# q split in the projections, low parts of weights kept in DRAM, attention's scores three units ahead: a hybrid decoder layer on one core

## The chip, the core and the metric

One Trainium2 chip, one of its cores. The time is device microseconds (us) of one execution; each figure is the median of several runs. TensorE (PE) multiplies matrices, with its weight load shown apart as PEld; VectorE (DVE), ScalarE (ACT) and GpSimd (POOL) work element by element; SyncE (SP) issues most DMAs. Each engine works through its own instructions in order.

## What is computed

A decoder layer over 2048 tokens of width 1024, in fp32:

```python
h = rmsnorm(x, g);  proj = h @ w_in                        # 1024 -> 3328
y_a = rwkv7_mixer(proj[:, :1792], ...)                     # 8 heads of 64, a recurrence in chunks
y_b = dilated_attention(q, k, v)                           # 8 heads of 64
x = x + concat(y_a, y_b) @ w_out
h = rmsnorm(x, ffn_g)
x = x + (silu(h @ w_gate) * (h @ w_up)) @ w_down           # 1024 -> 2816 -> 1024
return rmsnorm(x, final_g)
```

The attention runs three times per head and mixes the results by their log-sum-exp: in windows of 128 tokens, in windows of 512 over every 4th token, and over the whole sequence over every 16th. A query sees its own block of 128 keys and the one before it.

## The kernel before, in words

**Split products.** Each fp32 factor of a dense product is split into a high part `hi`, its value in the rounded format fp32r (`nc.scalar.copy`, ACT), and a low part `lo = raw - hi` (`tensor_tensor`, DVE). `three` (L234 to L237) makes hi x hi, lo x hi and hi x lo. For attention's scores a head's q (64 rows) is loaded twice, into partitions 0 to 63 and 64 to 127; `split_q` (L937) leaves its high part in partitions 0 to 63 and its low part in 64 to 127; k, loaded twice too, is split by `split_k` (L942) into two such tiles, so that two matmuls (L968, L969) make a score.

**Weights.** `Weights` (L186) serves pieces of 256 KB (128 x 512): `load` issues the raw load on SP (two raw buffers), `halve` splits it into `whi` and `wlo` (three buffers each), `take` hands out the next and keeps one more split ahead. A piece serves 12 matmuls. For `w_in` the first block of tokens also stores both parts in DRAM by POOL (L224), and the other three blocks read both back on SP (L205 to L211). All other weights, 416 pieces, are split every time: `w_out` once or more per block, `w_gate`, `w_up` and `w_down` in two passes over the tokens (`list_out`, `list_down`, L1400 to L1424), and `w_down` for the last two blocks from another `Weights` (`wds`).

**The order.** PE's instructions stay in the order of the program; the other engines' are ordered by a scheduler. The work is generators that yield costs in us. `drive` (L155) runs two of them against each other: each step of the first kind (rwkv, later attention) gives so many us to the second (the dense products). First the projections of four blocks of 512 tokens run with rwkv (`dense_in`, to about 820 us): 26 column tiles per block, of which tiles 14 to 17 are q, 18 to 21 k, 22 to 25 v. q and k go to DRAM, transposed, as `qT` and `kT`. Then attention runs against the output projections and the FFN.

**Attention.** The parts follow in `heads_b`: `attention(0)`, `branch3` (the 16-fold dilation, all blocks), `attention(1)` to `attention(3)`. `prep(h)` splits a head's operands: in `attention` q and k once in order (`q1`, `kh1`, `kl1`) and once reordered by 4 (`q2`, `kh2`, `kl2`), in `branch3` four blocks reordered by 16. A `Unit` is the score matmuls of one to four tiles into one of two PSUM buffers, a row maximum on DVE (L973, a subtraction of it follows in ACT's exponential, L978), transpositions into one PSUM buffer (L985), a copy from there by ACT or DVE in turn (L989), and the products with v (L999), copied out by ACT (L1004) and POOL (L1005). `flow` (L1012) puts the scores of a unit `ahead=2` units in front of its transpositions. Where there is a second buffer for k (`spare`, from the end of rwkv to the end of `attention(1)`) the next head's `prep` runs beside the units (`sides`), else between heads.

**The dense side.** `start` and `start_b` make output projections of blocks 0 to 3 from y_a and y_b: `put_by` (L1622) loads four tiles of x on SP, adds the products and stores the sums to `x1p`. Then `normed` (L1486) squares, scales and transposes block 0 in ten steps; each yields `HOLD` = 1.6 us to attention. `chunks0` and `chunks1` are the FFN of blocks 0 and 1, with `put_rest` (L1743) for the rest of the projections and `prepare` for blocks 2 and 3, whose gate products (`gate_up_pair`, 2300 to 2710 us) and down products (`downs`) come last; `next_acts` (L1982) loads the activations of a chunk from DRAM (`actD`) and splits them.

Of the kernel before, what the change touches and what calls it, by code (L numbers as in the profile page):

```python
# [9 lines left out]
F32 = mybir.dt.float32  # L10
# [31 lines left out]
def f32(ap):  # L42
    return ap.bitcast(F32)
# [3 lines left out]
def tile_hybrid_layer(  # L47
# [41 lines left out]
    qT = dram.tile([W, S], F32, name="qT")  # L89
# [96 lines left out]
    class Weights:  # L186


        def __init__(self, pool, srcs, raw_bufs, bufs, kept=None, again=0):


            self.pool, self.srcs, self.raw_bufs, self.bufs = pool, srcs, raw_bufs, bufs
            self.kept, self.again = kept, again or len(srcs)
            self.raw, self.ready, self.loaded, self.split = [], [], 0, 0

        def load(self):
            if self.loaded < self.again:
                src = self.srcs[self.loaded]
# [5 lines left out]
        def halve(self):  # L204
            if self.again <= self.split < len(self.srcs):  # L205
                parts = []
                for n, name in enumerate(("whi", "wlo")):
                    t = self.pool.tile([P] + list(self.srcs[self.split].shape[1:]), F32R, name=name, tag=name, bufs=self.bufs)
                    nc.sync.dma_start(out=f32(t), in_=self.kept[self.split % self.again, n])
                    parts.append(t)  # L210
                self.ready.append(tuple(parts))  # L211
                self.split += 1
            elif self.split < len(self.srcs):
                while self.loaded <= self.split:
                    self.load()
                raw = self.raw.pop(0)
                hi = self.pool.tile(list(raw.shape), F32R, name="whi", tag="whi", bufs=self.bufs)
                nc.scalar.copy(out=hi, in_=raw)  # L218
                lo = self.pool.tile(list(raw.shape), F32R, name="wlo", tag="wlo", bufs=self.bufs)
                nc.vector.tensor_tensor(out=lo, in0=raw, in1=f32(hi), op=ALU.subtract)  # L220
                self.ready.append((hi, lo))
                if self.kept is not None:
                    for n, t in enumerate((hi, lo)):
                        nc.gpsimd.dma_start(out=self.kept[self.split, n], in_=f32(t))  # L224
                self.split += 1
                while self.loaded < self.split + self.raw_bufs - 1 and self.loaded < self.again:
                    self.load()

# [17 lines left out]
    A_TAIL, A_START, A_FIRST, A_REST, HOLD = 0.5, 0.6, 1.14, 1.15, 1.6  # L246
# [87 lines left out]
    def new_suv():  # L334
# [3 lines left out]
    n_in = 2 * len(ORDER)  # L338
    w_parts = dram.tile([n_in, 2, P, 4, P], F32, name="w_parts")
# [3 lines left out]
            w_in2[half * 512 : (half + 1) * 512, ct * P : (ct + 1) * P].rearrange("(k p) n -> p k n", p=P)  # L343
            for _ in range(NB) for ct in ORDER for half in range(2)
        ],
        2, 3,
        w_parts, n_in,
# [38 lines left out]
    def dense_in():  # L386
# [58 lines left out]
        for b in range(nblocks):  # L445
            t0 = b * TB
            for at, ct in enumerate(ORDER):
# [26 lines left out]
                if ct < SHIFT_TILES:  # L474
# [28 lines left out]
                    got[b, ct] = o  # L503
                else:
                    o = sp.tile([P, TB], F32, name="qkv", bufs=1)
                    nc.scalar.copy(out=o, in_=pd)
                    if ct < 22:
                        dst = qT if ct < 18 else kT
                        r0 = ((ct - 14) % 4) * P
                        nc.scalar.dma_start(out=dst[r0 : r0 + P, t0 : t0 + TB], in_=o)  # L510
# [501 lines left out]
    def flow(units, ahead=2):  # L1012
# [83 lines left out]
    def attention(b):  # L1096
# [27 lines left out]
        def load_qk(h):  # L1124
            hs = slice(h * HD, (h + 1) * HD)
            rq = ap.tile([P, TB], F32, name="rq", tag="rq", bufs=2)
            load_dup(rq, qT[hs, t0 : t0 + TB])
# [929 lines left out]
```

## Time and profile before

| | |
|---|---|
| median of 3 runs | 2978.59 us (2977.94 to 2982.78) |
| profiled execution, its own time | 2977.17 us |
| its span, first to last instruction | 2975.1 us |
| mean granted TensorE clock | 0.98 |
| busy: PE, PEld | 2844.0 us (96%), 2333.9 us (78%) |
| busy: DVE, ACT, POOL | 2013.0 us (68%), 1329.4 us (45%), 610.0 us (21%) |
| DMA | 443.63 MB, mean 149 GB/s |

Busy time is that of instructions at work; waiting is not in it. Matmuls overlap, so one's duration is longer than the distance to the next. The granted clock is a share of 2.4 GHz; a mean of 0.9 is a stretch in which a fifth of the time was at 1.2 GHz. Waits are inferred: a line "A <- B" says that an instruction of A started late, and that what it last waited for was B. An engine may also be late without such a wait, when an instruction ahead of it in its queue is.

### The profile page before, as it was taken

What the parts mean: (1) busy time and instruction counts of PE and PEld (TensorE: products, weight loads), DVE (VectorE), ACT (ScalarE), POOL (GpSimd) and SP (SyncE); (2) the same over time, 40 slices, a digit from 0 to 9 for tenths busy, and PEclk for the clock granted to TensorE, in tenths of its full rate; (3) what the DMA queues carried; (4) which work ended last, traced back from release to release, by engine and by line L of the source; (5) the groups of instructions that cost most, each with busy time, mean ns of one, the idle gap of its engine ahead of it and who ended that gap; (6) DMA issues with size and microseconds to landing.
All of it is one profiled execution on the core that took longest, in us unless ns stands there. A gap on an engine that the chain in (4) does not pass through costs nothing. (4 is left out here: it accounts for less than half of the span.)

```text
span 2975.1 us, 47453 instructions
## 1 busy us (share of the span) xinstructions
PE 2844.0 (96%) x17193; PEld 2333.9 (78%) x17193; DVE 2013.0 (68%) x3970; ACT 1329.4 (45%) x2568; POOL 610.0 (21%) x801
## 2 busy tenths in 40 slices
PE   7999999999998888899999999999988999999998
PEld 6777777877777777788888888888776788887887
DVE  6776667667568877766666687665458777776443
ACT  5533423423326665665545566453244333334332
POOL 4443112113113222000111121111012333330001
PEclk9999999999998998899999999999999999999999
DMA  7673564553453787454445544443564322224443
GB/s 247 215 226 125 159 182 135 161 179 124 135 171 96 230 245 229 136 145 116 134 138 142 146 126 137 142 112 100 182 193 145 125 81 82 81 72 173 151 145 101
DMA packets 398158, 443.63 MB, mean 149 GB/s; under 512 B 31282, under 2 KB 264292, under 8 KB 397924
## 3 DMA queue, kind: packets, MB, share of 16 engines
q1 hardware_dynamic: 347124, 358.20, 40.3%
q0 software_dynamic: 18144, 59.78, 5.4%
q10 hardware_dynamic: 32656, 22.62, 2.5%
q8 instruction: 136, 2.23, 0.3%
q14 instruction: 98, 0.80, 0.1%
HBM read 351.03 MB, written 89.46 MB: 148 GB/s over the span
## 5 line engine op out<-in xcount | busy, mean ns | idle before, releaser
L220 DVE TENSOR_TENSOR wlo<-wraw,whi 128x512 fp32r<-128x512 f32 x468 | 331.1, 709 | 364.0 <-ACT whi L218 358.0
L218 ACT CAST whi<-wraw 128x512 fp32r<-128x512 f32 x468 | 289.2, 619 | 495.2 <-PE acc L237 217.7
L235 PE MATMUL pd<-h_hi,whi 128*128 128x512 f32 (+1 forms) x840 | 351.0, 418 | 2.0 <-DVE kx L483 0.9
L236 PE MATMUL pd<-h_lo,whi 128*128 128x512 f32 (+1 forms) x840 | 330.2, 393 | 1.0 <-DVE h_lo L403 0.8
L237 PE MATMUL pd<-h_hi,wlo 128*128 128x512 f32 (+1 forms) x840 | 330.4, 393 | 0.0
L1005 POOL COPY oo<-mx 128x2 f32<-128x2 f32 (+2 forms) x160 | 54.2, 345 | 767.3 <-DVE mx L973 644.6
L978 ACT ACTIVATE pr<-pr,mx 128x256 f32<-128x256 f32 (+1 forms) x416 | 162.7, 450 | 90.6 <-DVE mx L973 90.1
L235 PEld LDWEIGHTS pd<-h_hi,whi 128*128 128x128 f32 x840 | 159.5, 190 | 37.5 <-DVE kx L483 1.4
L237 PEld LDWEIGHTS pd<-h_hi,wlo 128*128 128x128 f32 x840 | 159.3, 190 | 35.4
L236 PEld LDWEIGHTS pd<-h_lo,whi 128*128 128x128 f32 x840 | 159.9, 190 | 28.6 <-DVE h_lo L403 2.6
L237 PE MATMUL mm<-z,wlo 128*128 128x512 f32 x440 | 174.7, 397 | 0.6 <-DVE wlo L1905 0.6
L236 PE MATMUL mm<-z,whi 128*128 128x512 f32 x440 | 174.4, 396 | 0.0
L235 PE MATMUL mm<-z,whi 128*128 128x512 f32 x440 | 174.2, 396 | 0.0
L999 PEld LDWEIGHTS po<-vv,pts 128*128 128x128 f32 x1008 | 152.6, 196 | 23.9 <-ACT oo L1004 4.3
L1924 DVE TENSOR_TENSOR part<-mm,part 128x512 f32<-128x512 f32 x154 | 105.7, 686 | 91.8 <-PE mm L237 91.8
L973 DVE CUSTOM_DVE_ANT_0 pr<-s_att,amask 128x256 f32<-128x256 f32 (+1 forms) x384 | 122.0, 361 | 47.5 <-PE s_att L969 46.8
L1903 ACT CAST whi<-raw 128x512 fp32r<-128x512 f32 x110 | 68.2, 621 | 189.9 <-PE mm L236 186.4
L235 PE MATMUL acc<-whi,a_hi 128*128 128x512 f32 x352 | 149.7, 425 | 3.0 <-DVE th L1521 1.3
L235 PE MATMUL acc<-whi,fh_hi 128*128 128x512 f32 x320 | 140.3, 438 | 11.0 <-ACT whi L218 5.1
L235 PE MATMUL pg<-fh_hi,whi 128*128 128x512 f32 x352 | 148.4, 422 | 0.6 <-DVE x L1538 0.6
L235 PE MATMUL pu<-fh_hi,whi 128*128 128x512 f32 x352 | 148.3, 421 | 0.0
L999 PE MATMUL po<-vv,pts 128*128 128x65 f32 x1008 | 144.5, 268 | 3.1 <-ACT oo L1004 3.1
(646 smaller groups left out, 7267.0 us busy)
## 6 DMA issues: line engine op xcount, KB each, us to landing
wraw<-in_w_down_dram SPq DMA_DIRECT2D x176, 256.0 KB, 2.8
whi<-w_parts SPq DMA_DIRECT2D x156, 256.0 KB, 2.7
wlo<-w_parts SPq DMA_DIRECT2D x156, 256.0 KB, 3.3
wraw<-in_w_gate_dram SPq DMA_DIRECT2D x88, 256.0 KB, 3.2
wraw<-in_w_up_dram SPq DMA_DIRECT2D x88, 256.0 KB, 2.8
rq<-qT SPq DMA_DIRECT2D x128, 128.0 KB, 3.3
wraw<-in_w_out_dram SPq DMA_DIRECT2D x64, 256.0 KB, 4.9
wraw<-in_w_in_dram SPq DMA_DIRECT2D x52, 256.0 KB, 3.7
```

What stands on the lines that cost most here:

```text
L218: nc.scalar.copy(out=hi, in_=raw)
L220: nc.vector.tensor_tensor(out=lo, in0=raw, in1=f32(hi), op=ALU.subtract)
L235: nc.tensor.matmul(ps, lhsT=lhs[0], rhs=rhs[0], start=first, stop=False)
L236: nc.tensor.matmul(ps, lhsT=lhs[0], rhs=rhs[1], start=False, stop=False)
L237: nc.tensor.matmul(ps, lhsT=lhs[1], rhs=rhs[0], start=False, stop=last)
L973: nc.vector.tensor_tensor_reduce(out=pr[:, g, :], in0=ps[:, g, :], in1=mask, scale=-0.125, scalar=-NEG, op0=ALU.add, op1=ALU.min, accum_ou ...
L978: nc.scalar.activation(out=pr[:, g, :], in_=pr[:, g, :], func=AF.Exp, scale=-1.0, bias=mx[:, g])
L999: nc.tensor.matmul(po[:, g, :], lhsT=pts[:, g, kb, :], rhs=vb[g][kb], start=(kb == 0), stop=(kb == kbs - 1))
L1005: nc.gpsimd.tensor_copy(out=o[:, :, OA:OW], in_=self.mxs[j])
L1903: nc.scalar.copy(out=hi, in_=raw)
L1924: nc.vector.tensor_tensor(out=out, in0=ps, in1=other, op=ALU.add)
```

## The change

- **q.** The projections split a q tile once (hi on ACT from PSUM, lo on DVE) and store both to `qS`. Attention loads the two halves into the two halves of the partitions; `split_q` is gone. The reordered copies, of q in all branches and of k's two parts in `attention`, are made by `nc.gpsimd.tensor_copy` (`turned_by`). k in `attention` is split once over the longer range. `branch3` still splits k in reordered form.
- **Low parts.** `Weights` takes for each piece where to store parts and where to read them. `w_in` stays as it was. Of the other pieces the first use of `w_gate`, `w_up`, `w_down` and the second half of `w_out` stores the low part by POOL (140 pieces); each later use (244 pieces) loads it on SP into the `wlo` buffer, without the DVE subtraction. The high part is still cast from the raw piece.
- **Order.** `flow` runs `ahead=3`; `HOLD` is 2.2, and the first norm yields three more of them after its first scaled half. `put_by` and `put_rest` load their residual rows after half of the pieces. `next_acts` loads two pairs of activations and then one more pair for every two that are split.

```diff
-    qT = dram.tile([W, S], F32, name="qT")
+    qS = dram.tile([2, W, S], F32, name="qS")
...
         def halve(self):
+            if self.split == len(self.srcs):
+                return
+            src, put, have = self.srcs[self.split]
+            shape = [P] + list(src.shape[1:])
+            hi = self.pool.tile(shape, F32R, name="whi", tag="whi", bufs=self.bufs)
+            lo = self.pool.tile(shape, F32R, name="wlo", tag="wlo", bufs=self.bufs)
+            for part, kept in zip((hi, lo), have or ()):
+                if kept is not None:
+                    nc.sync.dma_start(out=f32(part), in_=kept)
+            if not have or have[0] is None:
+                while self.loaded <= self.used:
                     self.load()
                 raw = self.raw.pop(0)
+                self.used += 1
                 nc.scalar.copy(out=hi, in_=raw)
+                if not have:
+                    nc.vector.tensor_tensor(out=lo, in0=raw, in1=f32(hi), op=ALU.subtract)
+                while self.loaded < self.used + self.raw_bufs - 1 and self.loaded < len(self.raws):
                     self.load()
+            for part, kept in zip((hi, lo), put or ()):
+                if kept is not None:
+                    nc.gpsimd.dma_start(out=kept, in_=f32(part))
...
-    A_TAIL, A_START, A_FIRST, A_REST, HOLD = 0.5, 0.6, 1.14, 1.15, 1.6
+    A_TAIL, A_START, A_FIRST, A_REST, HOLD = 0.5, 0.6, 1.14, 1.15, 2.2
...
+                elif ct < 18:
+                    hi = sp.tile([P, TB], F32R, name="q_hi", tag="qkv", bufs=1)
+                    lo = sp.tile([P, TB], F32R, name="q_lo", tag="kx", bufs=2)
+                    nc.scalar.copy(out=hi, in_=pd)
+                    nc.vector.tensor_tensor(out=lo, in0=pd, in1=f32(hi), op=ALU.subtract)
+                    r0 = (ct - 14) * P
+                    for n, part in enumerate((hi, lo)):
+                        nc.scalar.dma_start(out=qS[n, r0 : r0 + P, t0 : t0 + TB], in_=f32(part))
...
-    def split_q(hi, raw):
-
-        nc.scalar.copy(out=hi, in_=raw)
-        nc.vector.tensor_tensor(out=hi[HD:P], in0=raw[HD:P], in1=f32(hi[HD:P]), op=ALU.subtract)
+    def load_q_parts(dst, h, ts):
+
+        for n in range(2):
+            nc.sync.dma_start(out=f32(dst[n * HD : (n + 1) * HD]), in_=qS[n, h * HD : (h + 1) * HD, ts])
+
+    turned_by = nc.gpsimd.tensor_copy
...
-    def flow(units, ahead=2):
+    def flow(units, ahead=3):
...
-            split_q(q1, rq)
-            split_k(kh1, kl1, rk_all[:, TB - lead :])
+            turned_by(out=q1, in_=rq)
+            turned_by(out=q2, in_=rq.rearrange("p (i r) -> p r i", r=4))
+
+            kh, kl = place[:, 0, 0:n2], place[:, 1, 0:n2]
+            split_k(kh, kl, rk_all[:, TB - back :])
+            kh1, kl1 = kh[:, n2 - n1 :], kl[:, n2 - n1 :]
             yield 0.0
...
-            split_q(q2, rq.rearrange("p (i r) -> p r i", r=4))
-            split_k(kh2, kl2, rk_all[:, TB - back :].rearrange("p (n i r) -> p r n i", r=4, i=P))
+            for o, k in ((kh2, kh), (kl2, kl)):
+                turned_by(out=o, in_=k.rearrange("p (n i r) -> p r n i", r=4, i=P))
...
-                split_q(q3[:, :, b * n : (b + 1) * n], qs.pop(0).rearrange("p (i r) -> p r i", r=R3))
+                turned_by(out=q3[:, :, b * n : (b + 1) * n], in_=qs.pop(0).rearrange("p (i r) -> p r i", r=R3))
...
+    def list_one(key, src, again=False):
+
+        if not again:
+            srcs.append((src, None, None))
+        elif key in lows:
+            srcs.append((src, None, (None, lows[key])))
+        else:
+            lows[key] = dram.tile([P] + list(src.shape[1:]), F32, name=f"low{len(lows)}")
+            srcs.append((src, (None, lows[key]), None))
...
-    def normed(x1, b, h, hold):
+    def normed(x1, b, h, hold, lead=0):
...
                     loaded.append((ht, h, i, kq))
+                    if not i and not kq:
+                        for _ in range(lead):
+                            yield hold
                 yield hold
...
-            xts = []
-            for i in range(NT):
-                xt = fp.tile([P, W], F32, name="xh", tag="a_hi", bufs=6)
-                nc.sync.dma_start(out=xt, in_=x2[b * TB + i * P : b * TB + (i + 1) * P, ds_])
-                xts.append(xt)
             acc = [ps_f.tile([P, 512], F32, name="acc", tag="f") for _ in range(NT)]
             for n, k in enumerate(ks):
                 wh = wf.take()
+                if n == len(ks) // 2:
+                    xts = []
+                    for i in range(NT):
+                        xt = fp.tile([P, W], F32, name="xh", tag="a_hi", bufs=6)
+                        nc.sync.dma_start(out=xt, in_=x2[b * TB + i * P : b * TB + (i + 1) * P, ds_])
+                        xts.append(xt)
...
-        yield from normed(x1s[0], 0, hs_[0], HOLD)
+        yield from normed(x1s[0], 0, hs_[0], HOLD, 3)
...
+        load()
+        load()
         act = [(hi[:, f], lo[:, f]) for f in range(f1 - f0)]
...
-        for hi_f, lo_f in act:
+        for n, (hi_f, lo_f) in enumerate(act):
+            if n % 2 == 0:
+                load()
             nc.scalar.copy(out=hi_f, in_=f32(lo_f))
```

## Rows read from the trace of the kernel before

**Rows 1.** The page, first part: busy time, share of the span, instructions.
```profile
PE 2844.0 (96%) x17193; PEld 2333.9 (78%) x17193; DVE 2013.0 (68%) x3970; ACT 1329.4 (45%) x2568; POOL 610.0 (21%) x801
```
**Rows 2.** Windows by stage: length, busy us and instructions per engine, clock, DMA share, GB/s.
```profile
225.00:825.00 600.00, 590.29 (x4863) 470.35 (x4860) 403.12 (x816) 220.46 (x463) 132.12 (x153) 1.00 0.48 150
885.00:975.00 90.00, 70.36 (x756) 61.15 (x756) 76.81 (x209) 59.22 (x140) 33.39 (x49) 0.81 0.37 109
975.00:1125.00 150.00, 132.05 (x753) 111.17 (x753) 117.94 (x320) 97.07 (x206) 31.48 (x55) 0.94 0.81 243
1125.00:1275.00 150.00, 124.54 (x702) 108.07 (x701) 108.67 (x279) 100.24 (x193) 17.16 (x31) 0.89 0.59 175
1275.00:2175.00 900.00, 893.34 (x4741) 753.37 (x4740) 587.32 (x1210) 454.71 (x840) 115.08 (x175) 1.00 0.47 137
2175.00:2325.00 150.00, 134.32 (x585) 106.23 (x584) 108.55 (x173) 68.80 (x136) 31.66 (x32) 0.97 0.51 165
2325.00:2700.00 375.00, 375.00 (x1613) 303.03 (x1612) 276.88 (x345) 117.72 (x194) 137.07 (x116) 1.00 0.25 80
2700.00:2775.00 75.00, 70.14 (x294) 56.03 (x293) 44.05 (x69) 29.72 (x51) 2.18 (x4) 0.95 0.60 212
```
**Rows 3.** PE's waits from 885 to 1275: us in total, times, longest.
```profile
PE pt_att L985 <- DVE pts L989: 9.1, 6, 4.3
PE pt_att L985 <- ACT pts L989: 8.6, 6, 4.1
...
PE ptf L1445 <- DVE ht L1500: 5.5, 1, 5.5
PE s_att L968 <- ACT k_all L943: 4.7, 1, 4.7
PE s_att L968 <- DVE q2nd L940: 4.3, 1, 4.3
PE ptf L1445 <- DVE fh_lo L1448: 3.9, 4, 1.9
PE s_att L968 <- DVE mx L973: 3.6, 3, 1.3
```
**Rows 4.** The timeline, 1061 to 1067: start, us, engine, instruction, [idle before <- releaser].
```profile
1061.37 2.87 DVE L940 TENSOR_TENSOR q1st<-rq,q1st 64x512 fp32r<-64x512 f32 x2
1061.42 2.00 POOL L1363 TENSOR_TENSOR c<-oo,aog 128x512 f32<-128x512 f32 x1 [0.81 <-DVE oo L1358]
...
1064.61 1.27 ACT L978 ACTIVATE pr<-pr,mx 128x128 f32<-128x128 f32 x4 [5.10 <-DVE mx L973]
...
1066.41 0.66 PE L985 MATMUL pt_att<-ident,pr 128*128 128x128 f32 x4 [2.20 <-ACT pts L989]
```
**Rows 5.** The q subtractions (L940) from 885 to 1275: DVE busy us, clock, DMA.
```profile
885.00:1275.00 390.00, 51.01 (x51) 0.89 0.62 186
```
**Rows 6.** DVE's instructions by line and form, whole span: busy us, mean ns, idle before.
```profile
L220 DVE TENSOR_TENSOR wlo<-wraw,whi 128x512 fp32r<-128x512 f32 x468 | 331.1, 709 | 364.0 <-ACT whi L218 358.0 <-PE s_att L969 2.7 <-PE pt_att L985 1.9
...
L1905 DVE TENSOR_TENSOR wlo<-raw,whi 128x512 fp32r<-128x512 f32 x110 | 74.8, 680 | 0.1
...
L944 DVE TENSOR_TENSOR k_all<-rk_all,k_all 128x1024 fp32r<-128x1024 f32 x20 | 40.4, 2021 | 15.6 <-ACT k_all L943 15.6
```
**Rows 7.** POOL's instructions by line and form, whole span.
```profile
L224 POOL DMA_DIRECT2D w_parts<-wlo x52 | 28.9, 555 | 22.8 <-DVE wlo L220 10.4 <-DVE up L710 2.8 <-DVE M L714 2.6
...
L724 POOL MEMSET TAB<- 32x1024 f32 x8 | 7.6, 948 | 29.5 <-ACT TAB L723 29.2
```
**Rows 8.** The timeline at 2400, in the paired gate products.
```profile
2399.51 1.62 POOL L1896 TENSOR_TENSOR S<-S,raw 128x512 f32<-128x512 f32 x1
...
2400.51 1.18 DVE L1905 TENSOR_TENSOR wlo<-S,whi 128x512 fp32r<-128x512 f32 x1
```
**Rows 9.** PE's waits from 2215 to 2295.
```profile
PE acc L236 <- DVE wlo L220: 4.7, 3, 2.8
```
**Rows 10.** The page, sixth part: DMA issues, KB each, median us to landing.
```profile
wlo<-w_parts SPq DMA_DIRECT2D x156, 256.0 KB, 3.3
```

More of the change, by code (lines that the diff above doesn't have):

```diff
@@ L186, in tile_hybrid_layer, with __init__ @@
     class Weights:
-        def __init__(self, pool, srcs, raw_bufs, bufs, kept=None, again=0):
+        def __init__(self, pool, srcs, raw_bufs, bufs):
             self.pool, self.srcs, self.raw_bufs, self.bufs = pool, srcs, raw_bufs, bufs
-            self.kept, self.again = kept, again or len(srcs)
-            self.raw, self.ready, self.loaded, self.split = [], [], 0, 0
+            self.raws = [n for n, (_, _, have) in enumerate(srcs) if not (have and have[0] is not None)]
+            self.raw, self.ready, self.loaded, self.split, self.used = [], [], 0, 0, 0
         def load(self):
-            if self.loaded < self.again:
-                src = self.srcs[self.loaded]
+            if self.loaded < len(self.raws):
+                src = self.srcs[self.raws[self.loaded]][0]
                 raw = self.pool.tile([P] + list(src.shape[1:]), F32, name="wraw", tag="wraw", bufs=self.raw_bufs)
@@ L204, in halve @@
         def halve(self):
[L205 to L214, printed above, removed]
+            if self.split == len(self.srcs):
+                return
@@ L229, in take @@
+            self.ready.append((hi, lo))
+            self.split += 1
         def take(self):
@@ L1754, in put_rest @@
                 wh = wf.take()
+                if n == len(ks) // 2:
+                    xts = []
+                    for i in range(NT):
+                        xt = small("xr")
+                        nc.sync.dma_start(out=xt, in_=x1p[b * TB + i * P : b * TB + (i + 1) * P, ds_])
+                        xts.append(xt)
                 for i in range(NT):
@@ L1991, in next_acts, with load @@
             hi, lo = (pair_tile(t, 8) for t in tags)
-        for f in range(f0, f1, 2):
-            nc.sync.dma_start(
-                out=f32(lo[:, f - f0 : f - f0 + 2]), in_=actD[b, f : f + 2].rearrange("f p t -> p f t")
-            )
+        todo = list(range(f0, f1, 2))
+        def load():
+            if todo:
+                f = todo.pop(0)
+                nc.sync.dma_start(
+                    out=f32(lo[:, f - f0 : f - f0 + 2]), in_=actD[b, f : f + 2].rearrange("f p t -> p f t")
+                )
+        load()
+        load()
         act = [(hi[:, f], lo[:, f]) for f in range(f1 - f0)]
```

62 lines of the change are left out of this document (22 added, 40 removed).

## The prediction

> **What bounds the kernel now.** The profiled execution took 2977.17 us: a span of 2975.1 and 2.07 around it; the median of the runs shown, 2978.59, lies 1.4 above. The page's first part gives TensorE (PE) 2844.0 us of the span [rows 1], so at most 131 us can be won without less matmul work, and the change takes no matmul away. The windows by stage say where the 131 us lie [rows 2]. From 885 to 1275, where the first attention block and the dilation-16 branch run beside the output projections and the first norm, PE is idle for 19.64 + 17.95 + 25.46 = 63 us. There its granted clock is 0.81, 0.94 and 0.89, so it spent 2 x (0.19 x 90 + 0.06 x 150 + 0.11 x 150) = 85 us at 1.2 of 2.4 GHz. A stream at half clock lasts twice as long: up to 43 us more. From 1275 to 2175 PE is busy 893 of 900 us: nothing done for another engine there can show. From 2175 to 2325 it idles 16 us, from 2700 to 2775 5 us.
>
> PE's waits in that first stage name the engines behind it [rows 3]. The transposition waits 17.7 us for copies of the previous one out of its single PSUM buffer, the scores 12.6 us for their operands or PSUM (4.7 + 4.3 + 3.6), the norm's transpositions 9.4 us for DVE. One stretch of the timeline shows how [rows 4]: DVE spends 2.87 us on two q subtractions, the row maxima come after them, ACT stands 5.10 us at the exponentials, the copy behind these in ACT's queue comes late, and PE stands 2.20 us. So this stage hangs on the queues of DVE and ACT: DVE is busy 76.81 + 117.94 + 108.67 = 303 of 390 us.
>
> **The change, part by part.**
> *q split once.* In attention every head's q was split anew: 51 subtractions of 51.0 us on DVE in this stage [rows 5], each with a cast on ACT. All go. So does one of two k splits per head of attention(0), about 1 us by half of the 128x1024 row [rows 6], 8 us. Relief: 59 of DVE's 303 us, and about as much on ACT. It costs a subtraction and one more store for each of 16 q tiles in the projections: 16 x 0.709 = 11 us of DVE [rows 6], and ACT's queue can stand as long at the second store. PE is busy 590 of 600 us there [rows 2], and a tile's 24 matmuls cover the step: 375 us for 1613 matmuls [rows 2] make 0.232 us each, 5.6 us per tile. Without that cover it would cost those 11 us. I take 1.
>
> *POOL makes the reordered copies.* In place of the splits stand 64 POOL copies of 512 columns in this stage (four per head of attention(0) and of branch3). The trace has no such copy. The nearest rows are a memset of 1024 columns, 0.948 us, so 0.47 for 512 [rows 7], and a sum of two operands, 1.62 [rows 8]; I take 1.0, one operand read in strides lying between them, so 64 us; ends 30 and 104. POOL has room. The later blocks add 24 heads at 6 such copies' worth, 144 us in 900, where POOL was busy 115 [rows 2].
>
> POOL's work has a price on DVE, though [rows 8]. At 2400.51 a DVE subtraction with both operands in SBUF lasts 1.18 us while a POOL sum runs from 2399.51 for 1.62; undisturbed it takes 0.680 [rows 6]. It ended 0.56 us after the sum: it stood until POOL was done. The q subtraction in the timeline stretched in the same way, beside a POOL product of 2.00 us [rows 4]. If a quarter of the copies' 64 us stands in front of DVE, 16 us of the relief are given back: 59 - 16 = 43.
>
> The Trainium skill's GPSIMD Engine Reference (section 7) counts 2.9 cycles per element for reads in steps of over 8 bytes and 1.9 for others; at its 1.2 GHz that would be, as an estimate, 1.24 and 0.81 us, 76 us for the 64 copies. No row shows it.
>
> The Trainium skill's SBUF — State Buffer (section Terms) calls the port pair that the two engines share locked for a whole instruction, so that the loser fully blocks; the rows agree (1.18 us against 0.680). By that rule the extreme is a DVE held for all of POOL's time: a rival below.
>
> DVE's busy share falls from 303/390 = 0.78 to 260/390 = 0.67. Delay in a queue grows as busy over free time, 3.5 before and 2.0 after: some 45% less. Of the 30.3 us of operand and copy waits (17.7 + 12.6) that is **14 us**.
>
> *Three units ahead.* The scores' matmuls move one unit forward in PE's fixed order; nothing is added. ACT's and DVE's row work gets one unit more of time, the case of [rows 4]. It helps what the 45% covers, and some of the 23 us of idle time that [rows 3] do not name: **3 us**. The "pr" tiles (5 buffers) then hold five at most in attention(0), so DVE's maxima of a next unit can wait for the transpositions right before it; these stand ahead of it on PE, so this costs nothing.
>
> *The first norm.* After the first scaled half, attention now gets 4 x 2.2 = 8.8 us where it had 1.6: 7.2 more in front of a transposition that waited 5.5 us [rows 3]. I take that wait whole, and of 3.9 us behind it 2.5: **8 us**. The work comes from the full stage behind, which gets as much shorter.
>
> *Clock.* 14 + 3 + 8 = 25 of 63 us idle, 40%. The half-speed time follows the idle stretches: 40% of 43 is 17, and as PE often waits there anyway, half: **9 us**; ends 0 and 17.
>
> *Low parts kept.* 140 weight pieces are stored by POOL, and 244 are read later in place of a DVE subtraction of 0.709 us, 173 us of DVE. Nearly all of that lies where PE is full (893 of 900), so it is hidden and worth nothing. The exception is the preparation around 2250, where PE waits 4.7 us for a low part [rows 9]: **4 us**. The stores take 140 x 0.555 = 78 us of POOL [rows 7]; a store that is late holds one of three "wlo" buffers, so the subtraction three pieces on, then PE. The projections' first block does it with two stores per piece on the same three buffers. I take 1, ends 0 and 30.
>
> The reads are tighter. A low part's load waits on SP until its buffer is free, two pieces before its use: 24 matmuls, 5.6 us where no attention stands between. Such a load lands in 3.3 us [rows 10], which leaves 2.3. Behind it on SP stand the next raw piece, whose cast still has a piece more, and attention's loads, which come a head ahead. I take 2, ends 0 and 40.
>
> *Loads moved.* The residual rows of put_by and put_rest leave SP behind two weight pieces in place of ahead of all, so weights no longer stand behind their waits for buffers; they then have two pieces, 5.6 us without attention, until the sums. I take 2 for put_rest, where nothing else covers them, ends -3 and 8. The activation loads of the last stage come in pairs in place of all at once; around 2720 that relieves SP, but low parts now queue behind the token loads. PE idles 5 us there [rows 2]; I take 0, ends -5 and +8. Slower two-operand work on DVE under PE's full stages: 1.
>
> **Sum:** 14 + 3 + 8 + 9 + 4 = 38 us gained, 1 + 1 + 2 + 2 + 1 = 7 lost, 31 in all; 2977.2 - 31 = 2946.2, plus 1.4 for the median: 2947.6, say **2947**.
>
> **The rivals.**
> *POOL holds DVE (slower).* Same stage; price: 104 us of copies, all in front of DVE, against 59 saved; DVE's share rises from 0.78 to (303 + 45)/390 = 0.89. If DVE's 45 us reach PE, less 12 for norm and low parts and with the 7 lost: 2978.6 + 40 = 3019. It decides from 59/16 = 3.7 us of hold per head. For it: the stretched rows [rows 4, 8]. Against: a hold needs an operation with two SBUF operands at that moment, and the maxima read PSUM.
>
> *Low parts come late.* Without attention beside them run, by the order of the work, the 88 pieces of the last stage and 56 before it (put_rest 16, the last gates 20, two passes of down 20). Late by 0.3 us each they cost 43: 2978.6 - 31 + 43 = 2991; it decides from 31/144 = 0.22 us. For it: 2.3 us of slack. Against: the projections' later blocks load both parts of every piece in this way, with PE busy 590 of 600.
>
> *Relief that does not reach PE.* The transpositions have one PSUM buffer, so PE may stand at its copy whatever DVE's load. Then only norm, low parts and a little clock remain: 8 + 4 + 2 - 7 = 7: 2972. For it: 17.7 us of waits are at that buffer. Against: [rows 4], where the copy is late and not long. That the kept parts do what they say where PE is full, and so nothing for the time, is in the forecast already.
>
> *The clock comes back.* If two thirds of idle and half-speed loss go (42 + 29) and 4 for the low parts: 75 - 7 = 68, 2911. For it: idle and clock fall together in [rows 2].
>
> **How the numbers follow.** Forecast 0.59 (its own range 2925 to 2964), relief that stops short 0.16, clock 0.12, low parts late 0.07, POOL holding DVE 0.06. About 0.2% (6 us) is what a measurement can tell from no change, so up to 2972.6 is faster. Faster: 0.59 + 0.12 and three quarters of the 0.16 = 0.83; same: the other quarter and 0.03 of the late parts, 0.07; slower 0.10. The range 2908 to 2976 takes in the forecast's unknown costs and the relief that stops short, and leaves out both slower cases and a third of the clock's: less than 0.2.
>
> **What would show it.** Right: no q split on DVE or ACT, DVE under 275 us between the first attention block and the end of the norm, the copy waits at 17.7 us halved, the granted clock above 0.92 there, the wait for the scaled half gone, and the stage some 30 us shorter. Wrong: scores that wait for POOL, DVE subtractions above 0.9 us on average beside copies, PE waiting for "wlo" after 1275, or a new stall near 2720.

## The result, and the profile after

The kernel after takes **3005.32 us** (median of 4 runs, 3003.55 to 3007.19) where the kernel before took 2978.27 beside it: a ratio of **1.0097, 95% interval 1.0081 to 1.0113**. It is 29 us slower, where 31 us faster was forecast, and lies outside the range. The profiled execution has a span of 3001.5 us.

The page of the kernel after, first part and two lines of the sixth (KB each, median us to landing), to set beside [rows 1, 10]:

```profile
PE 2848.3 (95%) x17193; PEld 2335.7 (78%) x17193; DVE 1810.5 (60%) x3614; ACT 1202.7 (40%) x2440; POOL 887.8 (30%) x1101
...
wlo<-low SPq DMA_DIRECT2D x244, 256.0 KB, 3.4
...
low<-wlo POOLq DMA_DIRECT2D x140, 256.0 KB, 4.0
```

DVE lost 203 us of work and ACT 127, as the change says, and POOL gained 278. Nothing of that relief reached the time. The windows by stage of the kernel after, in the columns of [rows 2], say where it went:

```profile
885.00:975.00 90.00, 66.52 (x774) 58.04 (x774) 66.69 (x190) 43.54 (x120) 55.87 (x72) 0.82 0.36 107
975.00:1125.00 150.00, 131.04 (x777) 111.48 (x776) 110.16 (x311) 84.66 (x194) 53.81 (x77) 0.96 0.80 248
1125.00:1275.00 150.00, 129.20 (x727) 111.64 (x725) 88.39 (x264) 78.88 (x175) 56.08 (x79) 0.87 0.70 210
1275.00:2175.00 900.00, 875.42 (x4612) 736.17 (x4611) 487.07 (x990) 372.98 (x755) 306.19 (x374) 0.99 0.65 199
2175.00:2325.00 150.00, 136.00 (x603) 108.45 (x602) 76.24 (x130) 66.57 (x132) 28.65 (x36) 0.98 0.77 253
2325.00:2700.00 375.00, 374.12 (x1607) 301.84 (x1606) 277.00 (x349) 117.50 (x195) 139.59 (x119) 1.00 0.27 87
```

The stage for which the forecast was made, 885 to 1275, has 326.8 us of PE's work against 327.0 before: even. The stage called full is full no more: 875.42 of 900 us against 893.34, with a granted clock of 0.99 against 1.00. DVE has 100 us less to do there and POOL 191 us more. Instructions of PE by tile (duration min/median/max in ns, first and last start in us) date the loss:

```profile
L237 PE MATMUL pg<-fh_hi,whi x352: 387/397/494, 1247.1 to 2261.0; 128*128 128x512 f32 x176
...
L982 PE MATMUL s_att<-k2nd,q2nd x48: 272/277/415, 1143.5 to 1282.4; 128*128 128x128 f32 x48
...
L239 PE MATMUL mm<-z,wlo x440: 392/398/505, 2309.9 to 2737.8; 128*128 128x512 f32 x147
```

The first gate product comes 7 us later than before (1239.7), but the last score of this branch 15 us earlier (1297.9): as the change has it, attention is further on by then, and the two about cancel. The paired gate products begin 24 us late (2286.4 before) and end 23 us late. So nearly all of the loss arises between 1275 and 2300.

PE's waits there (us in total, times, longest) are many and small, and behind them stand DVE, ACT and the reads of low parts:

```profile
PE acc L237 <- DVE th L1546: 5.9, 2, 3.2
PE pg L239 <- DMA wlo<-low: 4.5, 4, 1.9
...
PE pg L237 <- DVE x L1563: 2.5, 2, 1.5
PE pg L237 <- ACT whi L220: 2.1, 1, 2.1
```

How the first two come late is seen in the timeline. Lines of POOL, DVE, ACT and PE of the kernel after, in two places:

```profile
1339.86 2.04 POOL L1163 CAST k2nd<-k2nd 128x1024 fp32r<-128x1024 f32 x1
...
1340.23 5.22 DVE L222 TENSOR_TENSOR wlo<-wraw,whi 128x512 fp32r<-128x512 f32 x1
...
1341.82 1.14 POOL L1154 CAST q_all<-rq 128x512 fp32r<-128x512 f32 x1
...
1342.87 2.01 POOL L1163 CAST k2nd<-k2nd 128x1024 fp32r<-128x1024 f32 x1
...
1346.10 0.49 PE L237 MATMUL acc<-whi,a_hi 128*128 128x512 f32 x1 [2.67 <-DVE th L1546]
...
1401.32 5.92 DVE L1353 TENSOR_TENSOR oo<-oo,c 128x520 f32<-128x520 f32 x1
...
1401.68 1.10 POOL L1154 CAST q_all<-rq 128x512 fp32r<-128x512 f32 x1
...
1402.71 3.96 POOL L1163 CAST k2nd<-k2nd 128x1024 fp32r<-128x1024 f32 x2
...
1407.27 0.63 ACT L1355 ACTIVATE c<-oo 128x512 f32<-128x512 f32 x1 [8.83 <-DVE oo L1353]
...
1409.07 1.14 ACT L220 CAST whi<-wraw 128x512 fp32r<-128x512 f32 x2
...
1409.74 0.49 PE L237 MATMUL pg<-fh_hi,whi 128*128 128x512 f32 x1 [2.05 <-ACT whi L220]
```

A subtraction that takes 0.69 us undisturbed lasts 5.22: it starts in the first of three POOL copies that follow each other without a gap, and ends 0.57 us after the third. POOL did not let DVE in between these instructions. PE waits 2.67 us for the product (L1546) that stands behind the subtraction in DVE's queue. At 1401 a sum of attention's merge (L1353, part of mixing a finished head's three results) stands 5.92 us in the same way, though it started 0.36 us before the first copy. ACT idles 8.83 us until that sum is done, the cast of a weight's high part stands behind that in ACT's queue, and PE waits 2.05 us for the cast. The Trainium skill's SBUF — State Buffer (section Terms) has the shared ports held for a full instruction; these two places show the hold outlasting the instruction, over a chain.

DVE does not always stand through the chain. Another place of the same trace:

```profile
1309.36 2.07 POOL L1163 CAST k_all<-k_all 128x1024 fp32r<-128x1024 f32 x1 [1.45 <-PE s_att L982]
...
1310.78 1.20 DVE L222 TENSOR_TENSOR wlo<-wraw,whi 128x512 fp32r<-128x512 f32 x1
...
1311.34 1.61 POOL L1154 CAST q_all<-rq 128x512 fp32r<-128x512 f32 x1
```

Here the subtraction ends 0.55 us after the first copy, and it is POOL's second that lasts longer, 1.61 us where its median is 1.11. From 885 to 2100 one of the weight subtractions or of the merge's last two sums stands at 26 such boundaries between two copies: at 15 POOL's next copy goes first, at 11 DVE does. With two units ahead (`e5_two_ahead`, below) it is 3 and 6. What decides between the two is not shown.

### The profile page after: what moved, and what is told of

Same layout as the page of the kernel before. It is cut to its first block, busy times and chain, and to the rows that moved or that the text cites. A ratio compares the mean times of both kernels' runs of the same rounds, so it can differ in the third digit from the quotient of the medians.

```text
span 3001.5 us, 47881 instructions
## 1 busy us (share of the span) xinstructions
PE 2848.3 (95%) x17193; PEld 2335.7 (78%) x17193; DVE 1810.5 (60%) x3614; ACT 1202.7 (40%) x2440; POOL 887.8 (30%) x1101
## 4 chain that ended last, share of the span: by engine, by line
PE 46%; DMA 8%; issue 4%; DVE 3%; ACT 2%; POOL 1%; SPq 1%; ACTq 0%; DVEq 0%; POOLq 0%
PE acc L237 5%; PE acc L238 5%; PE acc L239 5%; PE mm L239 5%; PE mm L238 5%; PE mm L237 5%; PE po L1012 2%; PE pu L237 2%; PE pu L239 2%; PE pu L238 2%; PE pg L237 2%; PE pg L239 2%; PE pg L238 2%; DMA wlo<-low 2%; PE pt_att L998 1%
## 5 line engine op out<-in xcount | busy, mean ns | idle before, releaser
L222 DVE TENSOR_TENSOR wlo<-wraw,whi 128x512 fp32r<-128x512 f32 x224 | 193.8, 866 | 198.2 <-ACT whi L220 193.1
L1563 DVE TENSOR_TENSOR x<-x,acc 128x512 f32<-128x512 f32 x108 | 71.8, 684 | 132.8 <-PE acc L239 132.4
L227 POOL DMA_DIRECT2D low<-wlo x140 | 76.4, 546 | 240.2 <-DVE wlo L222 211.4
```

The source lines that it names most:

```text
L227: nc.gpsimd.dma_start(out=kept, in_=f32(part))
L1563: nc.vector.tensor_tensor(out=x1[:, i, ds_], in0=x1[:, i, ds_], in1=acc[i], op=ALU.add)
```

## The experiments

Beside the experiments the kernel before had medians of 2970 to 2972 us, so all are compared as ratios to it; 0.1% is 3 us. The kernel after was timed once, in 4 executions, and not again beside the experiments. A difference of two ratios carries the uncertainty of both, some 0.2% or 6 us. A single profiled execution can differ by some us too, and small differences between traces are not read.

### First batch: one part undone at a time

**No kept low parts** (`e1_split_always`):

```diff
-        if not again:
+        if True:
             srcs.append((src, None, None))
```

> The kernel after with every weight piece outside the projections split on ACT and DVE again: no low part is stored or read; POOL's copies, the order and the moved loads stay. Theory L (the low parts' stores and reads cost the time: reads late on SP, raw pieces held behind them): most of the 27 us comes back, 2976 to 2985 us, PE busy over 890 of 900 us between 1275 and 2175, and no wait of PE for a low part's DMA. Theory P (POOL's copies hold DVE and come late for attention): 3000 to 3015, since 244 subtractions at about 0.9 us come back to a DVE that POOL already slows; the loss between 1275 and 2100 stays.

Measured: 1.0033 (1.0019 to 1.0048). 19 of the 29 us come back, but a third stays: neither theory alone. PE is busy 886.9 us from 1275 to 2175, between the 875.4 of the kernel after and the 893.3 before.

**Loads moved back** (`e2_loads_back`): the loads of put_by, put_rest and next_acts stand where they stood in the kernel before; for put_rest

```diff
+            xts = []
+            for i in range(NT):
+                xt = small("xr")
+                nc.sync.dma_start(out=xt, in_=x1p[b * TB + i * P : b * TB + (i + 1) * P, ds_])
+                xts.append(xt)
             acc = [ps_f.tile([P, 512], F32, name="acc", tag="f") for _ in range(NT)]
```

> The kernel after with the residual rows of put_by and put_rest loaded ahead of all pieces again, and the activations of the last stage all at once: the low parts, POOL's copies and the order of attention stay. Theory M (the moved loads are late for the sums in put_rest or hold the last stage): 2992 to 3000. Theory L: 3003 to 3008, no difference, or some us more, as more loads of one kind stand ahead of the low parts on SP. Theory P: 3005 within 3.

Measured: 1.0130 (1.0108 to 1.0151): 10 us *slower*. Theory M falls; the moved loads were a gain.

**The old order** (`e3_old_order`):

```diff
-    A_TAIL, A_START, A_FIRST, A_REST, HOLD = 0.5, 0.6, 1.14, 1.15, 2.2
+    A_TAIL, A_START, A_FIRST, A_REST, HOLD = 0.5, 0.6, 1.14, 1.15, 1.6
...
-    def flow(units, ahead=3):
+    def flow(units, ahead=2):
...
-        yield from normed(x1s[0], 0, hs_[0], HOLD, 3)
+        yield from normed(x1s[0], 0, hs_[0], HOLD)
```

> The kernel after with two units ahead and the first norm's old steps (1.6 us each, none added). Theory O (three units ahead hold too many tiles in attention's later blocks, or the work moved into the norm is missed later): 2985 to 3000. Theories L and P: the order gave a small gain before 1275 that the rest took back, so without it 3008 to 3018, with PE's waits for the norm's scaled half back.

Measured: 0.9996 (0.9980 to 1.0012). The whole loss comes back. That is theory O's direction, but more than its range (2985 to 3000, where 0.9996 of 2978 is 2977), and the opposite of what the two theories I had put first said.

**The old q** (`e4_old_q`): q is stored as it comes, `split_q` and the second `split_k` are back on ACT and DVE, and no copy is left on POOL.

```diff
-            turned_by(out=q1, in_=rq)
-            turned_by(out=q2, in_=rq.rearrange("p (i r) -> p r i", r=4))
+            split_q(q1, rq)
...
+            split_q(q2, rq.rearrange("p (i r) -> p r i", r=4))
```

> The kernel after with q stored as it comes and split in attention, k split twice, all on ACT and DVE as in the kernel before: no copy is left on POOL; the low parts, the order and the moved loads stay. Theory P: 2975 to 2990, and PE busy over 885 of 900 us between 1275 and 2175. Theory L: the loss between 1275 and 2100 stays and the relief before 1275 goes: 3008 to 3020.

Measured: 1.0051 (1.0031 to 1.0071): 14 us come back. The trace has theory P's sign, PE busy over 885 of 900 us from 1275 to 2175:

```profile
1275.00:2175.00 900.00, 891.25 (x4733) 752.03 (x4732) 506.45 (x1074) 450.13 (x837) 183.43 (x298) 1.00 0.67 208
```

Without a copy on POOL this stage is full again. What is left of the loss shows ahead of it: the granted clock from 885 to 1275 is 0.84 against 0.89, and the first gate product comes at 1257.7 against 1247.1.

Undoing three parts returned 19, 30 and 14 us of a loss of 29. So the parts do not add up; they share something. The traces named it: in the kernel after the merge's last two sums take 1.66 and 1.60 us on average, and about 0.70 with two units ahead. The next batch asked whether that is POOL's hold.

### Second batch: what the parts share

**Two units ahead alone** (`e5_two_ahead`):

```diff
-    def flow(units, ahead=3):
+    def flow(units, ahead=2):
```

> The kernel after with two units ahead and nothing else changed (the norm keeps its longer steps and the three added ones). Theory O3 (it is the third unit that costs: the merge of a finished head, four sums on DVE with two operands in SBUF, then falls beside POOL's copies for the next head and DVE stands through them): 2970 to 2978, all or nearly all of what the run with two ahead and the old norm steps gained, and the two last merge sums back at 0.70 us each, from 1.88 and 1.90. Rival N (it is the work moved into the norm): 3000 to 3008, merge sums still long.

Measured: 1.0005 (0.9989 to 1.0020). The third unit is what costs; the norm's steps are within 0.1% of nothing (against 0.9996 with the old steps).

**Copies on ACT** (`e6_copies_on_act`):

```diff
-    turned_by = nc.gpsimd.tensor_copy
+    turned_by = nc.scalar.copy
```

> The kernel after with the reordered copies made by ACT in place of POOL; three units ahead, the low parts and the moved loads stay. Theory H (POOL's copies hold DVE: a subtraction with two SBUF operands stands until a whole chain of copies has ended, up to 5.9 us): DVE's subtractions of weights back at 0.70 us on average from 0.895 and the merge sums at 0.70, and 2970 to 2988, though ACT gets about 220 us of copies more. Rival: POOL's hold is only a sign, the third unit or the reads on SP cost the time: 3000 to 3015, with ACT busier.

Measured: 0.9999 (0.9988 to 1.0011). With three units ahead and all else kept, the loss is gone: it takes the third unit *and* POOL's copies. DVE's weight subtractions and merge sums from 885 to 2100 (us in total, mean ns), first in the kernel after:

```profile
L222 DVE TENSOR_TENSOR wlo<-wraw,whi 128x512 fp32r<-128x512 f32 x172 | 154.6, 900 | 180.7 <-ACT whi L220 175.9 <-PE s_att L982 2.8 <-PE pu L239 1.6
...
L1353 DVE TENSOR_TENSOR oo<-oo,c 128x520 f32<-128x520 f32 x16 | 26.5, 1657 | 0.6
L1351 DVE TENSOR_TENSOR oo<-oo,c 128x520 f32<-128x520 f32 x16 | 25.6, 1601 | 0.4
```

with two units ahead:

```profile
L222 DVE TENSOR_TENSOR wlo<-wraw,whi 128x512 fp32r<-128x512 f32 x172 | 145.1, 844 | 153.6 <-ACT whi L220 151.4 <-DMA low<-wlo 1.9
...
L1351 DVE TENSOR_TENSOR oo<-oo,c 128x520 f32<-128x520 f32 x16 | 12.0, 751 | 0.2
L1353 DVE TENSOR_TENSOR oo<-oo,c 128x520 f32<-128x520 f32 x16 | 11.8, 736 | 0.7
```

and with the copies on ACT:

```profile
L222 DVE TENSOR_TENSOR wlo<-wraw,whi 128x512 fp32r<-128x512 f32 x172 | 118.9, 692 | 220.8 <-ACT whi L220 208.8 <-DMA xh<-in_x_dram 5.1 <-PE s_att L982 4.3
...
L1351 DVE TENSOR_TENSOR oo<-oo,c 128x520 f32<-128x520 f32 x16 | 11.2, 699 | 0.5
L1353 DVE TENSOR_TENSOR oo<-oo,c 128x520 f32<-128x520 f32 x16 | 11.2, 698 | 0.8
```

Against the last, DVE stood 35.7 + 15.3 + 14.4 = 65 us in these three groups in the kernel after, 28 us with two units ahead. With the third unit a head is finished one unit later; by these rows its merge then falls beside POOL's copies for another head.

**Both** (`e7_split_always_old_order`): the edits of `e1_split_always` and `e3_old_order` together.

> The kernel after without kept low parts and with two units ahead and the old norm steps: q split once, POOL's copies and the moved loads are what is left of the change. If low parts and order cost by separate ways, 3005 less 19 and less 30: 2956 to 2962. If both cost only because they add waits around the same held DVE, 2968 to 2975, no better than the old order alone.

Measured: 0.9989 (0.9976 to 1.0001). The prices do not add: once the merges are free of the chains, the low parts cost 2 us (0.9996 to 0.9989), which is within the uncertainty.

**The moved loads alone**, in the kernel before (`e8_loads_alone`): the reverse of `e2_loads_back`.

> The kernel before with the residual rows loaded after half of the pieces and the activations of the last stage in pairs, nothing else. Undoing this part in the kernel after cost about 10 us (1.0130 against 1.0097). Theory S (weight loads stand on SP behind loads that wait for buffers, in either kernel): 2962 to 2972 where before is 2971 to 2978, a ratio of 0.996 to 0.998. Rival (it helps only where low parts are read on the same queue): ratio 0.999 to 1.001.

Measured: 0.9974 (0.9963 to 0.9985). They gain 8 us there too.

### Third batch: what is left without POOL's chains

**Low parts not in the last stage, copies on ACT** (`e9_act_last_split`): the edit of `e6_copies_on_act` and

```diff
+    srcs[n_first:] = [(src, None, None) for src, _, _ in srcs[n_first:]]
     wf = Weights(fp, srcs[:n_first], 2, 3)
```

> The kernel after with the reordered copies on ACT, and with the weights of the last stage (w_down for the last two blocks) split on ACT and DVE again; the low parts of the stages before are still kept. Theory T (with POOL's hold gone, the kept low parts pay before 2300 and cost some 6 us in the last stage, where one late read makes PE wait 5.7 us): 2961 to 2966 where before is 2971, a ratio of 0.997 to 0.9985. Rival (the last stage makes up for that wait elsewhere): 0.9995 to 1.001, as with the copies on ACT alone.

**The same with two units ahead** (`e10_act_last_split_two`): this edit and that of `e5_two_ahead`.

> As the run before it in this batch, but two units ahead. If the third unit costs only by falling beside POOL's copies, it is worth something or nothing once ACT makes them: 0 to 4 us more than with three units, a ratio of 0.997 to 1.000. If the third unit costs by itself, this one is the faster by over 3 us.

**Three units ahead alone**, in the kernel before (`e11_three_ahead_alone`):

```diff
-    def flow(units, ahead=2):
+    def flow(units, ahead=3):
```

> The kernel before with three units ahead and nothing else. Theory H (three units are harmful only beside POOL's copies): ratio 0.997 to 1.001, merge sums at 0.70 us. Rival (three units hold what the next head needs, whatever POOL does): 1.003 to 1.010.

**Copies on ACT, no kept low parts** (`e12_act_split_always`): the edits of `e6_copies_on_act` and `e1_split_always`.

> The kernel after with the reordered copies on ACT and every weight split again: no low part is kept. Beside the first of this batch it prices the kept low parts before the last stage. If 173 us of DVE there are worth nothing, both are within 2 us; if DVE's relief shows (TensorE had some 12 us of progress more by 2710 us with the copies on ACT), this one is 4 to 10 us slower, a ratio of 0.9995 to 1.002. With ACT busier by the strided copies, it may also be no better than the kernel before.

Measured: 0.9988 (0.9977 to 0.9999), 0.9951 (0.9932 to 0.9970), 1.0013 (1.0002 to 1.0024) and 0.9964 (0.9951 to 0.9977). The first lies between the two ranges expected of it. The third unit costs 4 us in the kernel before and 11 us with all copies on ACT (0.9951 to 0.9988), so it is not only POOL that it collides with: this theory of mine was too narrow. And the low parts kept before the last stage cost 7 us (0.9988 against 0.9964) where I expected them to pay 4 to 10.

### Fourth batch: the length of the chain

**Copies on ACT, no kept low parts, two units ahead** (`e13_act_split_two`): those two edits and that of `e5_two_ahead`.

> The kernel after with the reordered copies on ACT, every weight split again and two units ahead: what is left of the change is q split once, the longer norm steps and the moved loads. If the third unit and the kept low parts each cost by themselves, as the runs before suggest (0.37% and 0.24 to 0.35%), ratio 0.992 to 0.995, the fastest so far. If both prices were those of one shared wait, 0.995 to 0.997. Against the moved loads alone (0.9974) it prices q split once with the norm's steps: my prediction's 14 + 8 us would make it 0.990, nothing would make it 0.997.

**Only k's copies on ACT, q's on POOL** (`e14_only_q_on_pool`): one line of the kernel after.

```diff
             for o, k in ((kh2, kh), (kl2, kl)):
-                turned_by(out=o, in_=k.rearrange("p (n i r) -> p r n i", r=4, i=P))
+                nc.scalar.copy(out=o, in_=k.rearrange("p (n i r) -> p r n i", r=4, i=P))
```

> The kernel after with the copies of k on ACT and those of q left on POOL; three units ahead, the low parts and the moved loads stay. If the length of an unbroken chain of POOL copies decides (5.0 us with k's copies around q's, at most 1.9 us with q's alone), most of the 28 us comes back: ratio 1.000 to 1.003, weight subtractions at 0.70 to 0.77 us on average. If every copy on POOL costs by its own length, q's make up some 100 of the 230 us, and 1.004 to 1.006 is left.

Measured: 0.9949 (0.9929 to 0.9969) and **0.9956 (0.9943 to 0.9970)**. The second goes further than either of its two expectations. That one line is worth 1.4%, 42 us: with it the change is 13 us faster than the kernel before, three units and low parts and all. POOL's copies in the kernel after, 885 to 2100, by form:

```profile
L1163 POOL CAST k_all<-k_all 128x1024 fp32r<-128x1024 f32 x40 | 87.1, 2199 | 36.2 <-PE s_att L982 34.5 <-PE s_att L981 1.3 <-ACT k_all L956 0.4
...
L1154 POOL CAST q_all<-rq 128x512 fp32r<-128x512 f32 x30 | 36.6, 1218 | 1.9 <-PE s_att L982 1.9
...
L1153 POOL CAST q_all<-rq 128x512 fp32r<-128x512 f32 x30 | 19.6, 653 | 24.8 <-PE s_att L982 20.9 <-DMA rq<-qS 2.1 <-DMA wraw<-in_w_up_dram 1.7
```

Eleven such rows make 221 us, of which k's four rows are 124. With these gone the chain that remains for a head of `attention` is 0.65 + 1.22 = 1.9 us by the means, the longest weight subtraction lasts 1.94 us where it lasted 5.22, and the longest of the two merge sums 2.04 where it lasted 5.92. DVE's lines of this kernel, in the form above, and the stage from 1275 to 2100, first here, then in the kernel after:

```profile
L222 DVE TENSOR_TENSOR wlo<-wraw,whi 128x512 fp32r<-128x512 f32 x172 | 123.6, 719 | 189.7 <-ACT whi L220 183.2 <-PE s_att L982 4.6 <-PE pg L239 1.3
```

```profile
1275.00:2100.00 825.00, 821.62 (x4399) 696.01 (x4398) 417.12 (x947) 440.03 (x767) 204.44 (x314) 1.00 0.66 205
```

```profile
1275.00:2100.00 825.00, 800.50 (x4270) 675.03 (x4269) 465.97 (x959) 350.19 (x717) 301.01 (x367) 0.99 0.64 195
```

PE is full again, 821.6 of 825 us against 800.5, although q's copies, 221 - 124 = 97 us, are still on POOL. DVE stands 12 us in place of 65 (4.7 on weights, 4.2 + 2.7 on the merges). 44% of the copies' time is left and 18% of the hold. As k's copies were both the longest and over half of the time, no run tells whether the length of a chain or the sum of the holds decides. The sum alone does not go with the loss: with every weight split (`e1_split_always`) these three groups still stood 57 us (weights 40.7, merges 8.7 + 7.2), and 19 of the 29 us had come back.

### Fifth batch: the last stage, and the best version

**q on POOL, k on ACT, last stage split, two units ahead** (`e15_q_on_pool_last_split_two`): the edits of `e14_only_q_on_pool`, `e9_act_last_split` (its weights alone) and `e5_two_ahead`.

> The kernel after with k's copies on ACT and q's on POOL, the last stage's weights split again and two units ahead. If the late low part of the last stage (5.6 us of PE's wait) and the third unit each still cost something: ratio 0.990 to 0.993. If with the short chains on POOL the third unit no longer costs, the same as the run with three units in this batch within 0.1%.

**The same with three** (`e16_q_on_pool_last_split`): without the edit of `e5_two_ahead`.

> As the other run of this batch, with three units ahead: against only q on POOL (0.9956) it prices the kept low parts in the last stage alone. If the one late read (5.6 us) is all of it, ratio 0.993 to 0.995; if the last stage makes it up elsewhere, 0.9945 to 0.997.

Measured: 0.9969 (0.9954 to 0.9984) and **0.9935 (0.9914 to 0.9955)**. The second is the fastest of all kernels: 2951.71 us, by the ratio 19 us under the kernel before. Against only q on POOL the kept low parts of the last stage cost 0.9956 - 0.9935 = 0.2%, 6 us, which is within the uncertainty of the two; with the copies on ACT it was 3 us (0.9999 to 0.9988), within it too. PE's waits after 2690 do show a late read, here in the kernel after:

```profile
PE acc L238 <- DMA wlo<-low: 6.4, 2, 5.6
```

and in the fastest one, where that stage's weights are split again:

```profile
PE acc L237 <- DVE x L1564: 0.7, 2, 0.4
PE acc L237 <- ACT whi L220: 0.7, 1, 0.7
PE acc L238 <- DVE wlo L222: 0.4, 1, 0.4
```

With short chains on POOL the third unit *gains* 10 us (0.9969 to 0.9935), which neither expectation had.

### Sixth batch: which load

**The residual rows alone** (`e17_residual_rows_alone`) and **the activations alone** (`e18_activations_alone`), each in the kernel before, with that half of the edit of `e8_loads_alone`.

> The kernel before with the residual rows of put_by and put_rest loaded after half of the pieces, nothing else. If it is these rows that made both moved loads together worth 0.26%: ratio 0.996 to 0.999. If it is the activations: 0.9990 to 1.0015.

> The kernel before with the activations of the last stage loaded in pairs, nothing else. In the traces the wait for a cast of a raw weight at the start of the last stage went from 4.7 to 2.1 us with both moved loads. If the activations are the cause: ratio 0.9970 to 0.9990. If it is the residual rows: 0.9990 to 1.0015.

Measured: 0.9997 (0.9986 to 1.0009) and 0.9979 (0.9967 to 0.9991). The activations in pairs are the gain, 6 us, and the residual rows nothing. PE's wait for a cast at the start of the last stage was 4.7 us before; with the activations in pairs:

```profile
PE acc L235 <- ACT whi L218: 2.6, 1, 2.6
```

That shows 2 of the 6 us; the traces do not place the rest.

## Why the prediction was wrong

**The step that failed first** is in its first paragraph: PE is busy 893 of 900 us from 1275 to 2175, and "nothing done for another engine there can show". That is true of a relief and false of a burden. The paragraph on POOL then put 144 us of copies into this stage because "POOL has room", and charged them 1 us, under "Slower two-operand work on DVE under PE's full stages". The stage lost 18 us of PE's work, and moving k's copies alone gave back more than the whole loss.

**The gains** of the sum did not come either. The first stage, which was to bring 14 + 3 + 8 and 9 us of clock, holds as much of PE's work as before (326.8 against 327.0 us) at the same clock. The nearest price of q split once and the norm's steps without POOL's copies is `e13_act_split_two` against the moved loads alone, 0.9949 against 0.9974: 7 us, with an uncertainty as large, where 14 + 8 were forecast. The 4 us for the wait around 2250 [rows 9] only changed their cause. PE's waits from 2090 to 2330, before and after:

```profile
PE acc L236 <- DVE wlo L220: 5.0, 4, 2.8
...
PE acc L238 <- DMA wlo<-low: 6.0, 4, 3.8
```

**POOL's hold**: its rate was about right and its shape wrong. A quarter of the copies' time was to stand in front of DVE, and 65 of 221 us did. But I counted only the first stage's 64 us, and took each hold for one instruction long, as [rows 8] show it. Chains of three copies can hold DVE five to six us at once, and PE shows it (2.67 us at 1346.10, 2.05 at 1409.74); where none of these instructions lasts over 2.04 us PE stays full. By the rule of the Trainium skill's SBUF — State Buffer (section Terms) on the shared ports, I had set the extreme at a DVE held for all of POOL's time; the share was 30%. The copies' own durations were met on the whole: 0.65 in order, 1.22 in strides and 2.20 for 1024 columns on average, against 1.0 per 512. By the Trainium skill's GPSIMD Engine Reference (section 7) I had 0.81 and 1.24 as an estimate: too long for the one in order, and right for the strided mean, which has copies in it that DVE holds up; the medians are 0.61 and 1.11.

**Three units ahead** was sized +3 us as a thing by itself. In this change it costs 27 us (1.0005 to 1.0097), and by the rows on the merge sums it does so by moving the merge beside the chains. Without k's copies there it gains 10.

**Low parts**: "hidden and worth nothing" was too good. Undoing them returned 19 us here, 10 with all copies on ACT (0.9999 to 0.9964) and 2 with the old order, so their cost hangs on the third unit more than on POOL's hold; how, the traces do not show. In the last stage they cost some 6 us, not clear of the uncertainty, within my ends of 0 to 40 though I took 2. That rival named the place, but it asked for 0.22 us on each of 144 pieces; what the trace has there is a read that PE waits 5.6 us for.

**Moved loads**: I took a loss of 2 on the residual rows, which measured nothing, and nothing on the activations, "ends -5 and +8", which gained 6, just past the end.

**The first norm**: the 5.5 us wait is gone from the trace, and the time does not show it: 1.0005 with the new steps, and 0.9996 without them, where the same wait is 10.5 us. So the 8 us had no place in the sum.

**What was right**: q's subtractions are gone, DVE is busy 265 us from 885 to 1275 (under 275, as forecast), and no score waits for POOL for more than 1.5 us. **What was not**: the copy waits in that stage, in the kernel after

```profile
PE pt_att L998 <- DVE pts L1002: 13.1, 8, 5.6
...
PE pt_att L998 <- ACT pts L1002: 8.1, 5, 3.9
```

rose to 21.2 us from 17.7 [rows 3] in place of halving, and the clock stayed at 0.89. So the queue rule that gave 14 us, busy over free time, has no support here; with fewer but longer holds in DVE's queue, the mean busy share says little.

**The rival that came nearest** was POOL holding DVE, at 0.06. As written it did not happen: it stood in the first stage, with DVE 0.89 busy, and DVE was 0.68 busy there. The mechanism was right and the stage wrong, and its price, all copies in front of DVE, was not what came: 65 of 221 us.

**Left open**: why the third unit costs 11 us with all copies on ACT (with every weight split too it is 4 us, 0.9949 to 0.9964, within the uncertainty), and why the low parts before the last stage cost 7 us there and nothing with two units (0.9951 and 0.9949). Moving the stores of low parts to another queue wasn't tried. Every edit also lets the scheduler order the instructions of ACT, DVE and POOL anew. No run holds that order fixed, so differences of 10 us and less may come from it and not from the part that was changed.

## What to carry to other kernels

A stage in which TensorE is full has nothing to win, but everything to lose: price a burden on another engine there, and by its longest unbroken stretch as well as by its sum. Work moved to POOL was cheap here in short pieces with gaps, as an unbroken run of POOL copies can be one stand of a DVE instruction with two operands in SBUF. Where undoing several parts of a change each returns most of its loss, look for what they share before dropping any: here one line, moved to another engine, turned 29 us lost into 13 gained.

## What the runs showed of the hardware

- A DVE subtraction or sum with two SBUF operands that meets POOL copies back to back can stand until the whole chain has ended: 5.22 and 5.92 us for work of 0.69 and 0.70, behind three copies. At 15 of 26 boundaries between two copies POOL went on, at 11 DVE came in between and the next copy took about 0.5 us longer. With q's copies alone the longest stood 2.04 us.
- DVE's sums with one operand in PSUM (L1563) are not held: 0.67 to 0.69 us from 885 to 2100, beside copies too.
- POOL copies 128x512 fp32 values in order in 0.61 us and read in strides in 1.11, and k's 128x1024 in 2.05 (medians; the means with DVE's delays are 0.65, 1.22 and 2.20). ACT does the same in 0.61, 1.12 and 2.06 on average.
